# A two-layer sequence trunk: an addition moved into a transfer, one pair's order and last operand, and the places of one set of sums

## The chip, the cores and the metric

The kernel runs on one core of one Trainium2 chip. The core has five engines that work side by side, each through its own instructions in order: TensorE (PE in the profile; its weight loads are PEld), VectorE (DVE), ScalarE (ACT), GpSimd (POOL) and SyncE (SP). SP's queue only issues transfers (DMA) here; POOL issues others. The metric is the device time of one execution in microseconds (us). All numbers of a trace are from one profiled execution and count from the start of its span.

## What is computed

The reference runs two layers over x (512 tokens, width 2048, float32). Cut to what matters here:

```python
def hybrid_layer(x, w_in, w_out, ...):
    h = rmsnorm(x, g_pre)
    z = h @ w_in                      # 2048 x 7184
    gq, gk, gv, gg, ga, aq, ak, av, ag = split_columns(z)
    # gated linear attention on gq, gk, gv with gate ga; its output times silu(gg)
    # chunked softmax attention on aq, ak, av; its output times silu(ag)
    y = concatenate([o_gla, o_att]) @ w_out
    return x + rmsnorm(y, g_post)
```

Nearly all of the time goes into `h @ w_in` and the product with `w_out`.

## The kernel before

**Precision.** Every float32 operand is split into a high part (a cast on ScalarE, "wh" for weights) and a low part (the difference, on VectorE, "wl"); three matmuls, high x high, high x low and low x high, make one product. `Job.high` (line 211) casts, `Job.low` (line 232) subtracts at line 237. Token operands are split by `split` (cast at line 108, difference at line 109).

**Blocks and pairs.** The columns of `w_in` are cut into 14 blocks of 512 (AG1 and AG2 are 264 wide, with the gate's columns). A block is multiplied directly by `std_gemm` (a "standard" pass, kind "std", eight chunks of the contraction), or two blocks together by `fast_gemm`, which uses the seven products of a Strassen-Winograd scheme, P1 to P7, over four chunks c = 0 to 3. The names in the order lists are product and chunk: "50" is P5 of chunk 0. For a chunk c and a pair (b0, b1) the weights come from four blocks: P1 loads b0's upper block into H; P5 loads b1's upper block into r and makes H = H + r; P6 loads b1's lower block (b22) and makes H = H + b22; P3 uses b22; P7 makes r = H - r with b0's upper block; P2 and P4 use b0's lower block. The additions are at line 221, P7's subtraction at line 223. P1, P2 and P4 take tokens as their left operand, P5, P6, P3 and P7 take sums of tokens, S1, S2, S4 and S3 (the table `LEFT`).

**Sums of tokens.** `make_sums` makes S1 to S4 for each chunk out of the tokens' quarters a11, a12, a21, a22: S1 = a21 - a22 and S3 = a11 - a21 (by `sub`, line 599), S2 (line 622) and S4 (line 625). `put` splits a sum into a tile and writes it to DRAM from POOL (line 610). In layer two S1 and S2 have tiles of their own (`HOMES`), S3 and S4 rotate through three staging tiles, and in layer one S1 has tiles of its own and the other three rotate through five; a tile is used again when its store has left. `put` ties the split's cast behind the last cast emitted so far (`last_cast`). In layer one `behind` also ties every S1 and S3 subtraction behind the last operand split emitted (`ends[-1]`). A later pair reads its sums back from DRAM into "sa" tiles, a ring of four (line 206), from SP; so does P4 with the quarter called A22.

**Order.** All jobs of the kernel stand in one list, `stream`. `ahead` prepares them in front of TensorE: loads up to five jobs ahead, casts up to four, low parts three. Side work is a list of generators, `tasks`; `pump` advances it by one step, and `Pace` pumps `rate` steps at each call. `std_gemm` calls its pace once for each chunk and token tile, `fast_gemm` once for each product and chunk. The program's order gives priorities; a scheduler at build time, with its own model of times, then fixes each engine's order, and `tc.issue_after(x)` keeps an instruction behind x on its engine. Rings: weights wait in "raw" (five tiles), "H" (four), "wh" (four), "wl" (three).

**Around the change, layer two (l = 1).** The layer runs: the standard pass of AG0 for token tiles 0 and 1; P2 and P1 of the values' pair (AV0, AV1), `PROD_FRONT`; the standard pass of AG0 for token tiles 2 and 3, from about 860 to 882 us, in which the sums are pumped at a rate of 0.9; the rest of the values' pair, `PROD_REST`, to about 944 us; then the narrow pair (AG1, AG2), `PROD_GATE`, to about 989 us; then the pair of queries and keys. For the values' pair of layer two, `Job.parted` is true, and its H tiles are the slots g4 to g7. S1 and S2 are taken from their tiles in this pair and in the narrow one (`home`); S3, S4 and A22 are read from DRAM.

**Layer one (l = 0).** The tokens arrive transposed and unnormalised; `first_operands` scales and splits them on VectorE (until about 69 us) while the standard passes of AG0, AG1 and AG2 run. `token_sums` follows in the list of tasks, beside AG1 and AG2, and the values' pair follows at about 97 us. The four tiles of the "H" ring first hold tokens and are free for this pair's weights when a chunk's last sum is done.

Of the kernel before, what the change touches and what calls it, by code (L numbers as in the profile page):

```python
# [23 lines left out]
NB_IN = 14  # L24
# [12 lines left out]
def hybrid_trunk(  # L37
# [98 lines left out]
    def order(text):  # L136
        return [("P" + z[0], int(z[1])) for z in text.split()]
# [3 lines left out]
    PROD_OUT = order("10 20 11 21 12 13 50 51 60 61 22 23 52 53 62 63 30 31 32 33 70 71 72 73 40 41 42 43")  # L141
    PROD_FRONT = order("20 21 22 23 10 11 12 13")
    PROD_REST = order("50 51 52 53 60 61 30 62 63 31 70 32 71 72 73 33 40 41 42 43")
    PROD_GATE = order("10 11 50 12 51 13 52 60 53 61 30 62 31 63 32 70 33 71 20 72 21 73 22 23 40 41 42 43")
    GATE_PAIR = (AG1, AG2)
    LEFT = {"P5": "S1", "P6": "S2", "P3": "S4", "P7": "S3", "P4": "A22"}
    SPARE = ("g12", "g13", "g16", "g17")
# [3 lines left out]
    class Job:  # L151
# [23 lines left out]
        def load(self):  # L175
            k, c, p, b0, b1 = self.kind, self.c, self.pair, self.b0, self.b1
            end = b0 >= NB_IN and k != "std"
            if end:
                c = OC[c]
            top, bottom = (c + 4, c) if end else (c, c + 4)  # L180
            mid = end and b0 == W23[0] and self.l < L - 1
            if k == "std":
                self.raw = self.fetch(rtile("raw", bufs=5), b0, c)
            elif k == "P1":
                h = slot(f"g{4 + c}", [2, 512]) if self.parted else rtile("H")
                p["H", self.c] = self.fetch(h, b0, top)
                last_h[0] = last_load[0]
            elif k == "P5":
                p["r", self.c] = self.fetch(rtile("raw", bufs=5), b1, top)
            elif k == "P6":  # L190
                p["r", self.c] = p["b22", self.c] = self.fetch(rtile("raw", bufs=5), b1, bottom)
            elif k == "P7":
                p["r", self.c] = p.pop(("t", self.c), None) or self.fetch(rtile("raw", bufs=5), b0, top)
            elif k == "P2" or (k == "P4" and (end or self.parted)):
                p["r", self.c] = self.fetch(rtile("raw", bufs=5), b0, bottom)
            sums = (so_d if end else sa_d)[self.l]
            src = sums.get((LEFT.get(k), c))
            if self.l == L - 1:
                home = k in ("P5", "P6") and b0 in (AV0, AG1)
            else:  # L200
                home = k == "P5" and b0 == AV0
            if src is not None and b0 != NB_IN and not home:
                until(lambda: k == "P4" or (id(sums), LEFT[k], c) in written)
                self.a = rtile("sa", (2, 512), F32R)
                with tc.issue_after(last_h[0]) if mid else nullcontext():
                    last_load[0] = nc.sync.dma_start(flat(self.a), src).ins
            if b0 == W23[0] and k == ("P6" if mid else "P5"):
                with tc.issue_after(last_h[0]):
                    p["t", self.c] = self.fetch(slot(f"a11{self.c}" if mid else SPARE[self.c], [2, 512]), b0, c + 4)

        def high(self):
            k, c, p = self.kind, self.c, self.pair
            if k == "std":
                src = self.raw
            else:
                h, r = p["H", c] if k != "P2" else None, p.get(("b22" if k == "P3" else "r", c))
                src = h if k in ("P1", "P5", "P6", "P4") else r
                early = k in ("P7", "P4") and self.b0 == W23[0] and self.l < L - 1
                with tc.issue_after(lows[-4 if early else -2]) if self.b0 >= NB_IN else nullcontext():
                    if k in ("P5", "P6") or (k == "P4" and (self.b0 >= NB_IN or self.parted)):  # L220
                        nc.vector.tensor_tensor(out=h, in0=h, in1=r, op=ALU.add)  # L221
                    elif k == "P7":
                        nc.vector.tensor_tensor(out=r, in0=h, in1=r, op=ALU.subtract)  # L223
            self.src = src
            self.wh = self.cut(rtile("wh", dtype=F32R))
            for z in self.parts():
                last_cast[0] = nc.scalar.copy(self.wh[:, z, :], src[:, z, :]).ins  # L227
# [98 lines left out]
    def std_gemm(l, blk, outs, chunks, operand, evac, rate=0.0, skip=0, lag=0):  # L326
        wide = W if blk == AG0 else N1
        pss = {o: ps_mm.tile([P, W], F32, tag="mm", name=nm("mm"))[:, :wide] for o in outs}
        pace = Pace(rate, skip)
        outs, n = list(outs), len(chunks)  # L330
        order = [(i, o) for i in range(n - lag) for o in outs]
        order += [(i, o) for o in outs for i in range(n - lag, n)]
        jobs = {}
        for i, o in order:
            c = chunks[i]
            if i not in jobs:
                jobs[i] = take(l, blk, "std", c)
            job = jobs[i]
            a = operand(o // 2, c)
            for kk in range(2):  # L340
                t = slice(kk * 256 + (o % 2) * P, kk * 256 + (o % 2 + 1) * P)
                ops = ((0, job.wh), (0, job.wl), (1, job.wh))
                for m, (part, rhs) in enumerate(ops):
                    nc.tensor.matmul(  # L344
                        pss[o], a(part, kk, o) if callable(a) else a[:, part, t], rhs[:, kk, :],
                        start=(i == 0 and kk == 0 and m == 0),
                        stop=(i == n - 1 and kk == 1 and m == 2),
                    )
            if o == outs[-1] and (i < n - lag or i == n - 1):
                ahead()  # L350
            if i == n - 1:
                evac(o, pss[o])
            pace()
# [240 lines left out]
    def make_sums(dst, tags, parts, home={}, behind=None):  # L594
        stage = [0]

        def sub(out, a, b):
            with tc.issue_after(behind()) if behind else nullcontext():
                nc.vector.tensor_tensor(out=out, in0=a, in1=b, op=ALU.subtract)

        def put(name, c, src):
            if (name, c) in home:
                op = A[name, c] = slot(home[name, c], [2, 512], F32R)
            else:
                tag = tags[stage[0] % len(tags)]
                op = rtile(tag, dtype=F32R) if tag == "H" else slot(tag, [2, 512], F32R)
                stage[0] += 1
            with tc.issue_after(last_cast[0]):
                split(op[:, 0, :], op[:, 1, :], src)
            nc.gpsimd.dma_start(dst[name, c], flat(op))  # L610
            written.add((id(dst), name, c))

        for c in range(4):
            a11, a12, a21, a22 = parts(c)
            yield
            sub(a22, a21, a22)
            put("S1", c, a22)
            yield
            sub(a21, a11, a21)
            put("S3", c, a21)  # L620
            yield
            nc.vector.tensor_tensor(out=a22, in0=a22, in1=a11, op=ALU.subtract)
            put("S2", c, a22)
            yield
            nc.vector.tensor_tensor(out=a12, in0=a12, in1=a22, op=ALU.add)
            put("S4", c, a12)
            yield

    def token_sums(l):
        tags, home = (("g10", "g16", "H"), HOMES) if l else (STAGE, HOME)  # L630
        return make_sums(sa_d[l], tags, lambda c: (full[0, c][:, 0, :], full[0, c][:, 1, :], full[1, c][:, 0, :], full[1, c][:, 1, :]), home, None if l else lambda: ends[-1])

    VT = ("g16", "g17", "g4", "g5", "g6", "g7", "g12", "g13")
    V, U = {}, {}
# [133 lines left out]
    def layer(l):  # L768
# [136 lines left out]
        if l:  # L905
            std_gemm(l, AG0, (0, 1), CO, operand_in, gate_evac(0), rate=1.3)
            roles.reverse()
            acc = {n: [ps_mm.tile([P, W], F32, tag="mm", name=nm("mm")) for _ in range(2)] for n in "YX"}
            fast_gemm(l, PAIRS[0], av_consume, rate=2.5, prod=PROD_FRONT, acc=acc)
            until(lambda: all((kh, 1, c) in A for kh in range(2) for c in range(4)))  # L910
            tasks.append(token_sums(l))
            std_gemm(l, AG0, (2, 3), CO, operand_in, gate_evac(0), rate=0.9)
            fast_gemm(l, PAIRS[0], av_consume, rate=1, prod=PROD_REST, acc=acc)
            drain()
            fast_gemm(l, GATE_PAIR, gate_consume, prod=PROD_GATE)
            tasks.append(load_forget_gate(l))
            tasks.append(forget_gate())
            act_table("natural_log_exp_and_others")
        else:
            fast_gemm(l, PAIRS[0], av_consume, rate=0.5)  # L920
# [658 lines left out]
```

## Time and profile before

| | us |
|---|---|
| three runs of the kernel before | 1628.22, 1624.83, 1628.18 |
| their median | 1628.18 |
| the profiled execution | 1626.38 |
| its span, first to last instruction | 1624.6 |

A second table gives where TensorE was idle for more than half a microsecond at a time in the stages of the edits:

| at, us | idle, us | ended by |
|---|---|---|
| 119.27 | 4.83 | ScalarE's cast of a weight tile (layer one, values' pair) |
| 891.83 | 3.14 | VectorE's low part of a weight tile (layer two, values' pair) |
| 970.22 | 0.84 | a transfer of S into "sa" (narrow pair) |
| 986.75 | 3.00 | a transfer of A22 into "sa" (narrow pair) |
| 989.50 | 0.75 | ScalarE's cast of a weight tile (queries and keys) |

How to read the rows: a timeline row has start, length, engine, line, operation, the written tile, "<-", the read tiles, sizes and a count, and in brackets the engine's idle time before it and what ended it. Tiles go by their tags ("g", "sa", "H"), buffer numbers left out. "mm" and "ax" are accumulators. A row of the view by stretches gives its length, the busy time and count of PE, PEld, DVE, ACT and POOL, the granted clock of TensorE, the mean busy share of the DMA engines and what they moved in GB/s. A matmul's row covers its pipeline, so the rows of successive matmuls overlap; their starts give the rate.

### The profile page before, as it was taken

The page shows a single profiled execution, that of the slowest core. Times are in us where ns is not written, and L with a number is a line of the kernel's source. Part 1 is how long each engine was busy: PE and PEld are TensorE (multiplying, and loading weights), DVE is VectorE, ACT ScalarE, POOL GpSimd, SP SyncE. Part 2 cuts the span into 40 slices and gives each one's busy share as a digit, 9 for nine tenths or more (in the row PEclk, how much of TensorE's full clock was granted, in tenths as well). Part 3 has the DMA queues.
Part 4 walks back from the last instruction along what each step waited for, and adds up shares of the span by engine and source line. Part 5 has one row for each costly group of instructions (what it writes and reads, how often), then busy time and mean ns, then how long its engine had stood idle before and what let it go on. Part 6 is the DMA issues. An engine that isn't in the chain of part 4 may idle for free.

```text
span 1624.6 us, 25125 instructions
## 1 busy us (share of the span) xinstructions
PE 1600.1 (98%) x9158; PEld 1378.9 (85%) x9158; DVE 1284.1 (79%) x1701; ACT 921.8 (57%) x1535; POOL 129.8 (8%) x202
## 2 busy tenths in 40 slices
PE   9989999999999999999999999999999999999998
PEld 7978999998888777888887798999988877788886
DVE  5977768678677877998989877686786778789887
ACT  7544445657455556665785545456575545465655
POOL 0220000000000001100121000000100000101001
PEclk9999999999999999999999999999999999999999
DMA  9697777685767768689868968866958677686887
GB/s 348 222 403 247 266 270 236 214 302 184 270 217 270 272 216 316 220 310 384 307 244 318 381 233 317 287 219 225 320 207 283 214 268 271 218 312 231 330 305 209
DMA packets 137228, 441.39 MB, mean 272 GB/s; under 512 B 14884, under 2 KB 27428, under 8 KB 137072
## 3 DMA queue, kind: packets, MB, share of 16 engines
q1 hardware_dynamic: 120528, 379.96, 67.0%
q0 software_dynamic: 16288, 59.53, 10.0%
q8 instruction: 72, 1.18, 0.3%
q14 instruction: 52, 0.43, 0.1%
q10 hardware_dynamic: 288, 0.30, 0.1%
HBM read 380.20 MB, written 61.62 MB: 272 GB/s over the span
## 4 chain that ended last, share of the span: by engine, by line
PE 85%; DMA 5%; issue 4%; DVE 4%; ACT 1%; POOL 0%; POOLq 0%; SPq 0%; DVEq 0%; ACTq 0%
PE mm L431 50%; PE mm L421 18%; PE mm L344 5%; PE ax L431 3%; DMA raw<-in_w_dram 3%; PE ax L1000 2%; DVE wl L237 2%; PE ax L1186 1%; PE ax L983 1%; PE ax L1158 1%; DMA sa<-S 1%; PE ax L963 1%; PE ax L962 1%; PE ax L961 1%; DMA sa<-A 1%
## 5 line engine op out<-in xcount | busy, mean ns | idle before, releaser
L431 PE MATMUL mm<-wh,sa 128*128 128x512 f32 (+1 forms) x1632 | 517.6, 388 | 5.2 <-DMA sa<-A 3.0
L227 ACT CAST wh<-H 128x1024 fp32r<-128x1024 f32 (+1 forms) x256 | 261.5, 1024 | 212.5 <-PE mm L431 88.7
L237 DVE TENSOR_TENSOR wl<-H,wh 128x1024 fp32r<-128x1024 f32 (+1 forms) x256 | 303.5, 1188 | 97.6 <-PE mm L431 35.8
L431 PEld LDWEIGHTS mm<-wh,sa 128*128 128x128 f32 x1632 | 303.0, 188 | 76.2 <-issue 13.0
L227 ACT CAST wh<-raw 128x1024 fp32r<-128x1024 f32 (+2 forms) x237 | 236.3, 1002 | 210.3 <-PE mm L431 85.6
L237 DVE TENSOR_TENSOR wl<-raw,wh 128x1024 fp32r<-128x1024 f32 (+2 forms) x237 | 272.8, 1154 | 63.3 <-PE mm L431 26.9
L431 PE MATMUL mm<-wl,sa 128*128 128x512 f32 (+1 forms) x816 | 313.9, 385 | 0.3 <-DVE wl L237 0.3
L421 PE MATMUL mm<-sa,wh 128*128 128x256 f32 x1280 | 237.7, 285 | 0.0
L431 PE MATMUL mm<-wh,a 128*128 128x512 f32 (+1 forms) x672 | 219.8, 392 | 5.9 <-ACT wh L227 5.9
L421 PEld LDWEIGHTS mm<-sa,wh 128*128 128x128 f32 x1280 | 200.5, 191 | 0.5
L421 PE MATMUL mm<-sa,wl 128*128 128x256 f32 x640 | 181.4, 284 | 0.6 <-DVE wl L237 0.6
L431 PEld LDWEIGHTS mm<-wl,sa 128*128 128x128 f32 x816 | 153.5, 188 | 29.5 <-DVE wl L237 1.1
L221 DVE TENSOR_TENSOR H<-H,raw 128x1024 f32<-128x1024 f32 (+1 forms) x144 | 170.3, 1188 | 1.0
L431 PEld LDWEIGHTS mm<-wh,a 128*128 128x128 f32 x672 | 125.4, 189 | 32.0 <-ACT wh L227 7.0
L431 PE MATMUL mm<-wl,a 128*128 128x512 f32 (+1 forms) x336 | 131.1, 391 | 0.3 <-DVE wl L237 0.3
L421 PEld LDWEIGHTS mm<-sa,wl 128*128 128x128 f32 x640 | 122.5, 191 | 0.8 <-DVE wl L237 0.8
L431 PE MATMUL mm<-wh,g 128*128 128x512 f32 (+1 forms) x384 | 115.8, 378 | 0.4 <-ACT wh L227 0.4
L475 POOL TENSOR_TENSOR sm<-sm,mhalf 128x2 f32<-128x2 f32 (+2 forms) x40 | 49.4, 1235 | 697.1 <-DVE sm L1010 388.3
L223 DVE TENSOR_TENSOR raw<-H,raw 128x1024 f32<-128x1024 f32 (+1 forms) x56 | 66.4, 1186 | 45.0 <-DMA raw<-in_w_dram 42.8
L421 PE MATMUL mm<-a,wh 128*128 128x256 f32 x512 | 96.7, 289 | 0.8 <-ACT wh L227 0.8
L381 ACT COPY ev<-mm 128x512 f32<-128x512 f32 (+1 forms) x112 | 64.0, 571 | 54.9 <-PE mm L431 39.5
L243 DVE TENSOR_TENSOR H<-H,raw 128x1024 f32<-128x1024 f32 (+1 forms) x48 | 56.7, 1181 | 42.0 <-DMA raw<-in_w_dram 41.5
(272 smaller groups left out, 2406.6 us busy)
## 6 DMA issues: line engine op xcount, KB each, us to landing
raw<-in_w_dram SPq DMA_DIRECT2D x291, 512.0 KB, 4.9
sa<-S SPq DMA_DIRECT2D x188, 512.0 KB, 4.5
H<-in_w_dram SPq DMA_DIRECT2D x60, 512.0 KB, 5.2
sa<-A SPq DMA_DIRECT2D x52, 512.0 KB, 5.7
sa<-oS SPq DMA_DIRECT2D x32, 512.0 KB, 5.4
S<-g POOLq DMA_DIRECT2D x30, 512.0 KB, 8.0
raw<-in_w_ag_dram SPq DMA_DIRECT2D x32, 264.0 KB, 4.2
oS<-g POOLq DMA_DIRECT2D x16, 512.0 KB, 4.5
```

Of the source, the lines that this page charges most:

```text
L221: nc.vector.tensor_tensor(out=h, in0=h, in1=r, op=ALU.add)
L223: nc.vector.tensor_tensor(out=r, in0=h, in1=r, op=ALU.subtract)
L227: last_cast[0] = nc.scalar.copy(self.wh[:, z, :], src[:, z, :]).ins
L237: last_low[0] = nc.vector.tensor_tensor(out=self.wl[:, z, :], in0=self.src[:, z, :], in1=self.wh[:, z, :].bitcast(F32), op=ALU.subtract).ins
L243: nc.vector.tensor_tensor(out=h, in0=h, in1=self.src, op=ALU.add)
L344: nc.tensor.matmul(pss[o], a(part, kk, o) if callable(a) else a[:, part, t], rhs[:, kk, :], start=(i == 0 and kk == 0 and m == 0), stop=(i ...
L381: last_copy[0] = nc.scalar.copy(e, src[t]).ins
L421: nc.tensor.matmul(dst, lhs[:, kk, f], a[:, part, tok], start=(fresh and kk == 0 and m == 0 and ft % 2 == 0), stop=(c == 3 and kk == 1 and ...
L431: last_mm[0] = nc.tensor.matmul(out_ps[t], a[:, part, tok], rhs[:, kk, :], start=(fresh and kk == 0 and m == 0), stop=(c == 3 and kk == 1 ...
L475: nc.gpsimd.tensor_tensor(out=out_r, in0=v, in1=mhalf[:, : v.shape[-1]], op=ALU.pow)
L961: nc.tensor.matmul(ps[:, :n], self.qh[:, t], self.kh[:, :n], start=True, stop=False)
L1000: nc.tensor.matmul(o, self.pt[i][:, j * P : (j + 1) * P], av[hd // 4, j // 2][:, j % 2, (hd % 4) * P : (hd % 4 + 1) * P], start=(j == 0), ...
```

## The change

Five edits, all of them in the order and the means of the same arithmetic.

1. In layer two's values' pair P5 no longer loads its block into a raw tile for VectorE to add; POOL issues a transfer that reads the block from DRAM and adds it into the H tile (`accum_op=ALU.add`). `Job.high` skips the addition for it.
2. `PROD_GATE`, the order of the narrow pair's 28 jobs, alternates P1 with P5, P6 with P3 and P7 with P2.
3. With each P5 of layer two's narrow pair the chunk's A22 operand is loaded into g4 to g7, and P4 takes it from there; P4 loads no "sa" tile in this pair any more.
4. In layer one the S1 and S3 subtractions of chunk 0 are tied to nothing, those of chunk 1 to the third last operand split, those of chunks 2 and 3 to the last as before.
5. The rate at which layer two's second standard pass pumps the sums goes from 0.9 to 1.3.

```diff
-    PROD_GATE = order("10 11 50 12 51 13 52 60 53 61 30 62 31 63 32 70 33 71 20 72 21 73 22 23 40 41 42 43")
+    PROD_GATE = order("10 50 11 51 12 52 13 53 60 30 61 31 62 32 63 33 70 20 71 21 72 22 73 23 40 41 42 43")
...
+            elif k == "P5" and self.parted:
+                h = p["H", c]
+                src = w[self.l, b1 - (b1 > AG1), top].rearrange("p (k n) -> p k n", k=2)
+                nc.gpsimd.dma_start(h, src, accum_op=ALU.add)
             elif k == "P5":
                 p["r", self.c] = self.fetch(rtile("raw", bufs=5), b1, top)
...
-            if src is not None and b0 != NB_IN and not home:
+            if b0 == AG1 and k == "P5":
+                p["a22", c] = slot(f"g{4 + c}", [2, 512], F32R)
+                nc.sync.dma_start(flat(p["a22", c]), sums["A22", c])
+            if b0 == AG1 and k == "P4":
+                self.a = p["a22", c]
+            elif src is not None and b0 != NB_IN and not home:
...
-                    if k in ("P5", "P6") or (k == "P4" and (self.b0 >= NB_IN or self.parted)):
+                    if k == "P6" or (k == "P5" and not self.parted) or (k == "P4" and (self.b0 >= NB_IN or self.parted)):
                         nc.vector.tensor_tensor(out=h, in0=h, in1=r, op=ALU.add)
...
-        def sub(out, a, b):
-            with tc.issue_after(behind()) if behind else nullcontext():
+        def sub(c, out, a, b):
+            with tc.issue_after(behind(c)) if behind and c else nullcontext():
                 nc.vector.tensor_tensor(out=out, in0=a, in1=b, op=ALU.subtract)
...
-            sub(a22, a21, a22)
+            sub(c, a22, a21, a22)
...
-            sub(a21, a11, a21)
+            sub(c, a21, a11, a21)
...
-        return make_sums(sa_d[l], tags, lambda c: (...), home, None if l else lambda: ends[-1])
+        return make_sums(sa_d[l], tags, lambda c: (...), home, None if l else lambda c: ends[-3 if c == 1 else -1])
...
-            std_gemm(l, AG0, (2, 3), CO, operand_in, gate_evac(0), rate=0.9)
+            std_gemm(l, AG0, (2, 3), CO, operand_in, gate_evac(0), rate=1.3)
```

More of the change, by code (lines that the diff above doesn't have):

```diff
@@ L630, in token_sums @@
         tags, home = (("g10", "g16", "H"), HOMES) if l else (STAGE, HOME)
-        return make_sums(sa_d[l], tags, lambda c: (full[0, c][:, 0, :], full[0, c][:, 1, :], full[1, c][:, 0, :], full[1, c][:, 1, :]), home, None if l else lambda: ends[-1])
+        return make_sums(sa_d[l], tags, lambda c: (full[0, c][:, 0, :], full[0, c][:, 1, :], full[1, c][:, 0, :], full[1, c][:, 1, :]), home, None if l else lambda c: ends[-3 if c == 1 else -1])
     VT = ("g16", "g17", "g4", "g5", "g6", "g7", "g12", "g13")
```

## The prediction

> **What bounds the kernel now.** I read the head of the page, then stretches of layer two's start, then what TensorE waited for in them.
>
> ```profile
> span 1624.6 us, 25125 instructions
> ...
> PE 1600.1 (98%) x9158; PEld 1378.9 (85%) x9158; DVE 1284.1 (79%) x1701; ACT 921.8 (57%) x1535; POOL 129.8 (8%) x202
> ```
>
> TensorE is the bound: it is idle for 24.5 us in all. No matmul is added or removed, so the change can win only idle time and the slow clock behind it. The stages of layer two's edits (columns: length; busy time of PE, PEld, DVE, ACT, POOL; granted clock; DMA share; GB/s):
>
> ```profile
> 840.00:862.00 22.00, 22.00 (x109) 18.47 (x107) 19.18 (x25) 17.41 (x32) 2.14 (x4) 1.00 0.56 209
> 862.00:880.00 18.00, 18.00 (x81) 14.89 (x81) 15.71 (x18) 10.52 (x13) 3.19 (x6) 1.00 0.89 288
> 880.00:910.00 30.00, 26.64 (x107) 20.72 (x106) 28.45 (x33) 16.43 (x25) 6.40 (x12) 0.94 1.02 387
> 910.00:944.00 34.00, 33.70 (x154) 27.47 (x153) 24.79 (x26) 13.04 (x16) 0.26 (x1) 1.00 0.97 363
> ...
> 960.00:1000.00 40.00, 35.38 (x266) 34.41 (x266) 28.89 (x53) 21.72 (x36) 4.92 (x9) 0.91 0.97 376
> ```
>
> **Stall A**, in the values' pair (880 to 910): 30.00 - 26.64 = 3.4 us idle, and 0.06 x 30 = 1.8 us lost to the clock: 5.2 us. **Stall B**, at the end of the narrow pair (960 to 1000): 4.6 us idle and 0.09 x 40 = 3.6 us of clock: 8.2 us. TensorE's rows name what ended them, in brackets behind the idle time:
>
> ```profile
> 891.83 0.50 PE L431 MATMUL mm<-wl,g 128*128 128x512 f32 x1 [3.14 <-DVE wl L237]
> ...
> 986.75 0.36 PE L431 MATMUL mm<-wh,sa 128*128 128x264 f32 x1 [3.00 <-DMA sa<-A]
> ...
> 989.50 1.22 PE L421 MATMUL mm<-a,wh 128*128 128x256 f32 x4 [0.75 <-ACT wh L227]
> ```
>
> In A VectorE is late; in B narrow P4's last operand, and after it the next pair's first cast. Layer one has a larger hole, **stall C**:
>
> ```profile
> 115.00:120.00 5.00, 0.73 (x2) 0.50 (x2) 0.75 (x1) 1.82 (x2) 0.00 (x0) 0.75 1.03 420
> 120.00:125.00 5.00, 5.00 (x15) 3.77 (x14) 4.95 (x5) 2.31 (x4) 0.00 (x0) 0.56 0.78 282
> ```
>
> That is 4.3 us idle and (0.25 + 0.44) x 5 = 3.4 us of clock, 7.7 us.
>
> **The addition by transfer** takes four additions (line 221) from VectorE and four loads from SP's queue, and gives POOL four accumulating transfers.
>
> ```profile
> 868.03 1.23 DVE L221 TENSOR_TENSOR g<-g,raw 128x1024 f32<-128x1024 f32 x1 [1.01 <-DMA raw<-in_w_dram]
> 869.17 0.69 DVE L109 TENSOR_TENSOR g<-g,g 128x512 fp32r<-128x512 f32 x1
> 869.77 0.68 DVE L625 TENSOR_TENSOR H<-H,g 128x512 f32<-128x512 f32 x1
> ```
>
> From start to start a wide operation takes 1.14 us and a half one 0.60, so 4 x 1.14 = 4.6 us leave VectorE, and the wait of 1.0 us for the first load with them. VectorE is the engine that is late in A, busy 28.45 of 30 us. The trace has no accumulating load. The nearest rows are the accumulating stores at the kernel's end (issue in ns, then landing in us: least, median, most). The outer ends are the plain stores A<-sa of 840 to 862 us and S<-g of 85 to 122 us, where the transfers were full:
>
> ```profile
> L1431 POOL DMA_DIRECT2D out_dram<-a x2: 852/893/934, 1602.3 to 1609.1; - x2
> DMA to landing us min/median/max: 5.4/5.8/7.7
> DMA to landing us min/median/max: 2.9/2.9/3.2
> DMA to landing us min/median/max: 10.3/13.7/15.4
> ```
>
> A landing takes 2.9 to 15.4 us; I take 5.8, the same kind of transfer. The four tiles are free once P1's low parts are made, before the standard pass, and P5 reads them after it: eight chunks of 12 matmuls at 18.00/81 = 0.222 us, 21 us. From 840 to 862 us POOL is busy 2.14 of 22 us and the transfers 0.56: 22 x 209 = 4.6 MB, of 9.3 MB that the 420 GB/s above would move. Even counted twice (4.2 MB) the additions fit. Cost: nothing, hidden by the standard pass. If they are issued only among the sums' stores, P5's first cast is up to 15.4 - 5.8 = 9.6 us later. The Trainium skill, "SBUF — State Buffer" (SBUF: two separate sides), speaks against moving loads to POOL: VectorE's two-port modes keep GpSimd from writing descriptors, and in its example 620 ns become 3100. By that four transfers would take POOL some 10 us longer, an estimate, and the sum would lose up to 10 us; the row above, 0.9 us to issue, shows no such growth, and the sum keeps nothing of it.
>
> **The rate of 1.3.** Sixteen paces pump 20.8 steps in place of 14.4, so five sums (S4 of chunk 2, all of chunk 3) come before the pair's rest: 5 splits and 3 additions, 8 x 0.60 = 4.8 us of VectorE, moved forward. Against it stand the 4.6 us taken out and 18.00 - 15.71 = 2.3 us idle at 862 to 880, so it fits. It also ends a knot: `put` ties a sum's cast behind the last cast emitted, four products ahead. P5's last product needs chunk 3's S1, which so far came behind the cast of P3's first product; now it comes behind that of P5's third. What tightens is staging, three tiles for eight S3 and S4. ScalarE waited once for a store to leave, while stores landed in (second row) 7.1 us:
>
> ```profile
> 882.39 0.62 ACT L108 CAST g<-g 128x512 fp32r<-128x512 f32 x1 [2.31 <-DMA S<-g]
> DMA to landing us min/median/max: 3.7/7.1/8.5
> ```
>
> Such waits may recur; casts run three products (8 us) ahead, which covers them. Of A's 5.2 us I count 4.1 as won, and set 1.6 us against new small waits in a stage whose transfers are 0.97 to 1.02 busy. Bounds: 5.2 won, 10 lost.
>
> **The narrow pair.** P4's four operands leave the ring of "sa" tiles for g4 to g7, which the values' P4 frees with its low parts; SP's issue waits for the last of these, then loads 40 us earlier than now:
>
> ```profile
> 934.92 1.21 DVE L237 TENSOR_TENSOR wl<-g,wh 128x1024 fp32r<-128x1024 f32 x1
> 976.52 0.33 SPq L206 DMA_DIRECT2D sa<-A  x1
> 977.20 3.10 SPq L172 DMA_DIRECT2D H<-in_w_dram  x3
> DMA to landing us min/median/max: 10.5/11.4/12.7
> 988.41 1.04 ACT L227 CAST wh<-H 128x1024 fp32r<-128x1024 f32 x1
> ```
>
> The 2.1 MB (5.0 us at 420 GB/s) now load near 936 us. Queued behind them on SP are narrow P5's and P6's weights, due products later. They vanish from in front of the next pair's H tiles, whose landing (fourth row) falls from 10.5 to 5.5 us: 977.2 + 5.5 + 1.04 of cast = 983.7 us. TensorE, without the 4.6 - 0.75 = 3.9 us lost before 988.75 us, would be through at 984.9. So the next late thing is that H tile, just in time. I keep 1.5 us of idle and clock: 6.7 us won (bounds 0 and 8.2). Alternating P1 with P5 and P7 with P2 moves no work, and one product still lies between each eviction and the next writer of its bank; it costs nothing beside a VectorE that is busy 28.89 of 40 us.
>
> **The untied subtractions.** Four half operations, 2.4 us, may pass VectorE's last operand splits. Stall C's chain:
>
> ```profile
> 106.02 0.62 ACT L108 CAST g<-H 128x512 fp32r<-128x512 f32 x1 [2.93 <-DMA S<-g]
> 108.45 0.33 SPq L172 DMA_DIRECT2D H<-in_w_dram  x1
> 119.27 1.22 PE L431 MATMUL mm<-wh,a 128*128 128x512 f32 x2 [4.83 <-ACT wh L227]
> ```
>
> The last sum waits for a staging store, then TensorE for the H tile that the sum frees. Earlier sums of chunks 0 and 1 put stores ahead of the jam, but a VectorE that is nearly full lets little through. Bounds: 2.4 us lost, 7.7 won; I take 1.5 won, nearer to nothing.
>
> **Sum.** -4.1 + 1.6 - 6.7 - 1.5 = -10.7 us. The profiled execution took 1626.4 us (1.8 beside the span); the runs are 1624.83 to 1628.22, median 1628.18. 1626.4 - 10.7 = 1615.7, and 0.8 for the higher median: **1616.5**.
>
> **Rivals.** *Layer one's hole closes too* (0.12): stores moved out of the jam shorten two landings in a row, and C gives 6 more: about 1610. For: 420 GB/s there, nothing to spare. Against: VectorE is full before it.
>
> *Only the narrow pair wins* (0.16): A moves to staging or a late operand; -6.7 + 1 gives 1621.
>
> *The transfers bind* (0.12): 862 to 944 us moved 18 x 288 + 30 x 387 + 34 x 363 = 29.1 MB. If the 363 GB/s of the last stretch is all there is, that takes 80 of the 82 us, nothing shrinks, and the time is 1625. Against: 420 GB/s in layer one, at which it takes 69 us. The Trainium skill, "SBUF — State Buffer" (A bandwidth-pool intuition that's wrong), gives some 358 GB/s between HBM and a core; by that this rival would be the result, at about 81 us. The 387 and 420 speak against it.
>
> *Slower* (0.14): the sums outrun staging, and ScalarE, which works in order, holds the casts behind them. S3 of chunk 3 reuses a tile after two stores, the first at 865.56 us; P5's fourth cast may stand behind it and is due three products (8.0 us) after P5's start:
>
> ```profile
> 865.56 0.53 POOL L610 DMA_DIRECT2D S<-g  x1 [9.22 <-DVE g L109]
> 881.99 0.39 PE L431 MATMUL ax<-wl,g 128*128 128x512 f32 x1
> ```
>
> The cast is done at 865.6 + 2 x (landing + 1.5) + 1.6 against 890.0. At 7.1 us nothing waits, at 15.4 TensorE waits 11.0 us, at 18, with the additions in the same queue, 16.2, each plus 2 of clock. A, B and C together lose 5.2 + 6.7 + 1.5 = 13.4, so it is slower from 15.6 us on; at 18 it gives +4.8, 1632. Against: 7.1 here.
>
> Only the untied edit can fail to act (C unchanged, 1.5 us).
>
> **Numbers.** Forecast 0.46, its own range 1612 to 1621. 0.2%, 3.3 us, is about what a measurement can tell from no change. Faster: 0.46 + 0.12 + 0.15 of the narrow-only case = 0.73; same 0.13; slower 0.14. Range 1609 to 1628, from the closed hole to no gain; the slower case and 0.04 below stay out.
>
> **What would show it.** Accumulating loads on POOL before 862 us and P5's additions gone from line 221; no wait on wl near 890; no sa<-A at the narrow end, the next cast within 1 us; S<-g landings near 8 us. Landings of 15 us, or additions issued among the sums' stores, would make it wrong.

## The result and the profile after

| | us |
|---|---|
| the changed kernel, median of eight runs | 1618.3 (1616.13 to 1621.13) |
| the kernel before beside it, median of eight | 1625.26 (1622.78 to 1628.22) |
| ratio | 0.9956, 95% interval 0.9944 to 0.9968 |
| the profiled execution of the changed kernel | 1617.69, span 1615.9 |

It is faster by 7 us (5.2 to 9.1 us by the interval); the forecast was 1616.5 in 1609 to 1628. From one profiled span to the other it is 1624.6 - 1615.9 = 8.7 us. In the changed kernel lines stand nine further down once the additions are passed: 221 is 230, 227 is 236, 237 is 246, 421 is 430, 431 is 440, 206 is 215.

The view by stretches of the changed kernel (columns as before: length; busy time of PE, PEld, DVE, ACT, POOL; granted clock; DMA share; GB/s):

```profile
100.00:125.00 25.00, 20.36 (x80) 15.10 (x79) 18.22 (x17) 10.87 (x14) 2.20 (x4) 0.93 0.90 361
...
840.00:862.00 22.00, 22.00 (x107) 18.41 (x106) 20.18 (x26) 16.73 (x29) 5.75 (x8) 1.00 0.95 251
862.00:880.00 18.00, 18.00 (x81) 14.93 (x80) 15.71 (x20) 11.47 (x17) 4.81 (x9) 1.00 1.01 396
880.00:910.00 30.00, 29.66 (x130) 23.90 (x129) 26.77 (x29) 16.64 (x23) 5.10 (x10) 1.00 1.02 385
910.00:944.00 34.00, 34.00 (x185) 29.54 (x184) 26.38 (x32) 14.50 (x20) 0.00 (x0) 1.00 0.91 348
...
960.00:1000.00 40.00, 35.56 (x277) 34.74 (x276) 31.49 (x52) 20.38 (x31) 4.91 (x9) 0.96 0.84 310
```

Set these beside the rows of before. Stall A is gone: 0.3 us idle at 880 to 910 in place of 3.4, the clock 1.00 in place of 0.94. Stall B is not: 4.4 us idle at 960 to 1000 in place of 4.6. What ends it is another thing; TensorE's longest waits over the whole span (the view of waits: us in total, times, longest):

```profile
PE mm L440 <- ACT wh L236: 5.1, 6, 3.3
PE mm L430 <- ACT wh L236: 3.9, 1, 3.9
```

The 3.0 us for sa<-A have left the list. The 3.9 us on line 430 are new: the query and key pair's first product waits for the cast of its first H tile. The 3.3 on line 440 is layer one's stall C, 4.8 before.

### The profile page after: what moved, and what is told of

Same layout as the page of the kernel before. It is cut to its first block, busy times and chain, and to the rows that moved or that the text cites. A ratio compares the mean times of both kernels' runs of the same rounds, so it can differ in the third digit from the quotient of the medians.

```text
span 1615.9 us, 25135 instructions
## 1 busy us (share of the span) xinstructions
PE 1595.7 (99%) x9158; PEld 1377.2 (85%) x9158; DVE 1279.2 (79%) x1697; ACT 920.6 (57%) x1535; POOL 134.9 (8%) x206
## 4 chain that ended last, share of the span: by engine, by line
PE 87%; DMA 4%; issue 4%; DVE 3%; ACT 1%; POOL 1%; POOLq 0%; SPq 0%; DVEq 0%; ACTq 0%
PE mm L440 51%; PE mm L430 19%; PE mm L353 5%; PE ax L440 3%; PE ax L1009 2%; DMA H<-in_w_dram 2%; DMA raw<-in_w_dram 2%; PE ax L1195 1%; DVE wl L246 1%; PE ax L992 1%; PE ax L1167 1%; PE ax L972 1%; PE ax L971 1%; PE ax L970 1%; DMA S<-g 0%
## 5 line engine op out<-in xcount | busy, mean ns | idle before, releaser
L440 PE MATMUL mm<-wh,sa 128*128 128x512 f32 (+1 forms) x1600 | 510.3, 390 | 1.7 <-DMA sa<-S 1.1
L440 PEld LDWEIGHTS mm<-wh,sa 128*128 128x128 f32 x1600 | 297.7, 188 | 71.3 <-issue 7.7
L440 PE MATMUL mm<-wl,sa 128*128 128x512 f32 (+1 forms) x800 | 309.3, 387 | 0.0
L440 PE MATMUL mm<-wh,g 128*128 128x512 f32 (+1 forms) x416 | 120.5, 368 | 0.5 <-ACT wh L236 0.4
```

Source lines behind the costliest of these rows:

```text
L440: last_mm[0] = nc.tensor.matmul(out_ps[t], a[:, part, tok], rhs[:, kk, :], start=(fresh and kk == 0 and m == 0), stop=(c == 3 and kk == 1 ...
```

## The experiments

All kernels compute the same result; only the order, the means or the place of work differ. Each ratio is against the kernel before on the same chip.

### The parts of the values' pair, and the first layer, each alone

**The addition by transfer alone** (edit 1):

```diff
+            elif k == "P5" and self.parted:
+                h = p["H", c]
+                src = w[self.l, b1 - (b1 > AG1), top].rearrange("p (k n) -> p k n", k=2)
+                nc.gpsimd.dma_start(h, src, accum_op=ALU.add)
...
-                    if k in ("P5", "P6") or (k == "P4" and (self.b0 >= NB_IN or self.parted)):
+                    if k == "P6" or (k == "P5" and not self.parted) or (k == "P4" and (self.b0 >= NB_IN or self.parted)):
```

> Edit 1 alone: only P5's addition by transfer, everything else as before. Theory 1 (the four additions on VectorE were what made it late): TensorE's idle time in the values' pair of layer two, 3.4 us before and 0.3 us with the whole change, falls to 1 us or less, ratio about 0.997. Rival (the knot: chunk 3's S1 was emitted behind the cast of P3's first product, whatever VectorE has to do): 2.5 us or more of it stays, ratio 0.999 to 1.0. Both: the accumulating loads are issued before 862 us and land in 3 to 8 us.

Measured 1621.22, ratio 0.9973 (0.9964 to 0.9983). The view by stretches of that kernel:

```profile
880.00:910.00 30.00, 29.57 (x131) 24.17 (x130) 26.21 (x29) 18.39 (x25) 5.86 (x11) 1.00 1.02 385
...
960.00:1000.00 40.00, 33.87 (x254) 32.90 (x253) 27.44 (x50) 19.08 (x32) 4.93 (x9) 0.91 0.95 365
```

Stall A's idle time goes with this edit alone, 0.4 us in place of 3.4, and the rival falls. The clock reads 1.00 here in place of 0.94, but it also reads 1.00 in the profiles of edit 5 alone and of edit 4 alone (below), which keep 1.8 and 3.8 us of idle time in these 30 us; that the clock's 1.8 us hang on the stall is not shown. The four loads are issued from 843.9 to 855.4 us and land in 5.5 to 9.4 us, a little later than the 3 to 8 expected. At the narrow end 6.1 us are idle in this profile in place of 4.6, and the wait for sa<-A is 4.0 us, 3.0 before. The two later kernels with this edit and the old narrow pair have 4.3 and 4.2, so that the stall is handed on is not shown.

**The rate alone** (edit 5):

```diff
-            std_gemm(l, AG0, (2, 3), CO, operand_in, gate_evac(0), rate=0.9)
+            std_gemm(l, AG0, (2, 3), CO, operand_in, gate_evac(0), rate=1.3)
```

> Edit 5 alone: the sums at a rate of 1.3, P5 still adds on VectorE. Theory 1: 4.8 us of sums come in front of an already late VectorE, so the idle time in the values' pair stays at 3 us or grows to 5, ratio 1.0 to 1.002. Rival (the knot): the idle time falls to 1 us or less, ratio about 0.997.

Measured 1625.01, ratio 0.9999 (0.9986 to 1.0012): nothing. The stretches:

```profile
880.00:910.00 30.00, 28.18 (x121) 21.82 (x120) 28.93 (x33) 17.67 (x24) 6.41 (x12) 1.00 1.02 384
910.00:944.00 34.00, 32.34 (x147) 26.19 (x146) 24.22 (x25) 13.00 (x17) 0.26 (x1) 1.00 0.95 358
```

Idle time from 880 to 944 us is 1.82 + 1.66 = 3.5 us, against 3.4 + 0.3 before: the stall is cut in two and moved, and the rival (the knot) falls.

**Both** (edits 1 and 5, as in the two diffs above):

> Edits 1 and 5 together, without the narrow pair's and without layer one's. Both theories: idle time in the values' pair about 0.3 us as in the whole change, some 5 us with the clock; whether the narrow pair hands it on is open: its operand transfers then meet the same jam earlier. Ratio about 0.997; near 1.0 if the stall only moves to the narrow pair's end (idle there above 6 us).

Measured 1619.57, ratio 0.9961 (0.9949 to 0.9972), and the idle time at 880 to 910 is 30.00 - 29.89 = 0.1 us. The interval overlaps that of the addition alone, so the rate's share, 1.7 us by the medians, is not settled.

**The untied subtractions alone** (edit 4):

```diff
-        def sub(out, a, b):
-            with tc.issue_after(behind()) if behind else nullcontext():
+        def sub(c, out, a, b):
+            with tc.issue_after(behind(c)) if behind and c else nullcontext():
...
-home, None if l else lambda: ends[-1])
+home, None if l else lambda c: ends[-3 if c == 1 else -1])
```

> Edit 4 alone: layer one's subtractions of chunks 0 and 1 untied. If the hole at 100 to 125 us shrank through this edit, its idle time is 4.6 us in place of 6.6, the queries' and keys' pair starts at 182.6 us in place of 184.5, and the new idle 0.6 us at 50 to 75 us is there too; ratio about 0.999. Rival: layer one's gain is not this edit's, idle stays at 6.6 us, ratio 1.0.

Measured 1622.62, ratio 0.9991 (0.9978 to 1.0003), some 1.5 us with an interval that just holds zero; the medians lie 3.0 us apart. The stretch of layer one, the kernel before and then this one:

```profile
100.00:125.00 25.00, 18.41 (x67) 13.01 (x66) 18.22 (x19) 9.74 (x13) 3.28 (x6) 0.86 0.98 390
```

```profile
100.00:125.00 25.00, 21.19 (x79) 15.61 (x78) 18.10 (x20) 11.03 (x13) 2.64 (x5) 0.86 0.93 373
```

TensorE works 21.19 of these 25 us, 18.41 before: 2.8 us less idle. Some goes back at 50 to 75 us, where a new wait of 0.6 us for an activation of ScalarE stands (line 344, before the sums' stage). The queries' and keys' pair of layer one starts at 183.6 us, 184.4 before: 0.8 us in this profile, less than the 1.9 expected. All profiles together settle what the interval leaves open: without edit 4 (the kernel before and the runs of edit 1, of edit 5, of both and of edits 2 and 3) that pair starts at 184.3 to 185.5 us, and in the seven profiles with it at 182.0 to 183.6. The means are 2.1 us apart, so the edit wins about 2 us.

### The narrow pair

**Edits 2 and 3 alone:**

```diff
-    PROD_GATE = order("10 11 50 12 51 13 52 60 53 61 30 62 31 63 32 70 33 71 20 72 21 73 22 23 40 41 42 43")
+    PROD_GATE = order("10 50 11 51 12 52 13 53 60 30 61 31 62 32 63 33 70 20 71 21 72 22 73 23 40 41 42 43")
...
+            if b0 == AG1 and k == "P5":
+                p["a22", c] = slot(f"g{4 + c}", [2, 512], F32R)
+                nc.sync.dma_start(flat(p["a22", c]), sums["A22", c])
+            if b0 == AG1 and k == "P4":
+                self.a = p["a22", c]
```

> The kernel before with the alternation and the A22 loads into free slots alone. Theory (the next pair's S1 loads and raws take the place of the A22 loads ahead of its H tiles): the waits sa<-A (3.0 us) go, a wait on the cast of the next pair's first H tile of 3 to 4.5 us stands in their place, 960 to 1000 us keeps 4 to 5 us of idle time, the H tiles land in 11 to 13 us, and the time is within 0.2% of before (1622 to 1627). Rival (the prediction's step: H lands in 5.5 us, 6.7 us won): idle time there under 1.5 us, 1619 or less. The idle time at 880 to 910 stays near 3.4 us by both.

Measured 1625.09, ratio 0.9993 (0.9984 to 1.0002). TensorE's rows and the stretch:

```profile
991.43 0.74 PE L426 MATMUL mm<-a,wh 128*128 128x256 f32 x4 [3.20 <-ACT wh L232]
```

```profile
960.00:1000.00 40.00, 35.80 (x282) 35.17 (x281) 28.94 (x55) 22.45 (x39) 5.04 (x10) 0.96 0.91 331
```

No wait on sa<-A is left; one of 3.2 us on the next pair's first cast stands in its place, and 4.2 us are idle. The theory held.

**The changed kernel without them** (the same two pieces put back):

> The changed kernel with the narrow pair put back (the old alternation, A22 loaded into the ring as before); the addition by transfer, the rate and the untied subtractions stay. Theory (the narrow edits do win something once the pair before them runs ahead, though less than 6.7 us): waits of 1.5 to 4 us on sa<-A and sa<-S at 960 to 1000 us, the query-key pair starts at 983 to 985 us in place of 981, and the time is 1619 to 1621.5, 2 to 3.5 us above the changed kernel. Rival (they win nothing, as alone): within 1 us of the changed kernel, 1617 to 1618.7.

Measured 1618.02, ratio 0.9946 (0.9930 to 0.9962); the changed kernel, run once more on another chip, has 0.9951. The rival held: the narrow pair's two edits win nothing in the changed kernel either. Its stretch and its longest wait there (1.0 us more stand on sa<-S):

```profile
960.00:1000.00 40.00, 35.76 (x273) 35.33 (x273) 29.19 (x50) 20.98 (x32) 4.92 (x9) 0.91 0.91 350
```

```profile
PE mm L435 <- DMA sa<-A: 3.2, 1, 3.2
```

4.2 us idle with the edits taken out, 4.4 with them in. Only the name of the last comer differs.

### What took the place of the A22 loads

SP's queue says why. In the kernel before, with A22 in the ring of "sa" tiles (timeline of SP: start, length until the last of x is issued, what):

```profile
974.63 1.46 SPq L172 DMA_DIRECT2D raw<-in_w_dram  x2
976.52 0.33 SPq L206 DMA_DIRECT2D sa<-A  x1
977.20 3.10 SPq L172 DMA_DIRECT2D H<-in_w_dram  x3
980.65 0.33 SPq L206 DMA_DIRECT2D sa<-S  x1
```

The query and key pair's S1 loads (sa<-S) come behind its H loads, since P4's operands hold the ring. In the changed kernel:

```profile
961.84 0.39 SPq L215 DMA_DIRECT2D sa<-S  x1
963.46 1.05 SPq L172 DMA_DIRECT2D raw<-in_w_dram  x2
964.61 0.38 SPq L215 DMA_DIRECT2D sa<-S  x1
966.55 1.56 SPq L172 DMA_DIRECT2D raw<-in_w_dram  x2
968.17 0.42 SPq L215 DMA_DIRECT2D sa<-S  x1
968.69 0.39 SPq L172 DMA_DIRECT2D raw<-in_w_dram  x1
969.17 0.39 SPq L172 DMA_DIRECT2D H<-in_w_dram  x1
969.67 0.42 SPq L215 DMA_DIRECT2D sa<-S  x1
```

The ring is free, and three of the four S1 loads, 1.6 MB that the second product wants, go out ahead of the first H tile, which the first product wants. The four A22 loads that left were 2.1 MB. The chain of waits of the changed kernel (start, length, what) goes through that H tile:

```profile
968.05 0.96 PE mm L440 x8
...
969.17 10.56 DMA H<-in_w_dram
...
979.82 1.05 ACT wh L236
```

To test it, **S1 is tied behind the H loads**, the changed kernel otherwise:

```diff
-                with tc.issue_after(last_h[0]) if mid else nullcontext():
+                later_s1 = self.l == L - 1 and b0 == QK01 and k == "P5"
+                with tc.issue_after(last_h[0]) if mid or later_s1 else nullcontext():
                     last_load[0] = nc.sync.dma_start(flat(self.a), src).ins
```

> The changed kernel, with the S1 loads of layer two's first query-key pair (4 loads of 512 KB) tied behind the loads of that pair's H tiles. Theory (they displaced H): the first H load is issued several us earlier or lands in 8 us or less in place of 12.3, the wait of the first product on its first cast falls from 3.9 us to 0 to 2, the idle time at 960 to 1000 us from 4.4 to 1 to 3 us, and the time is 2 to 4 us under that of the changed kernel (1614 to 1616.5 beside it). Rival (the four raw tiles ahead of H, or the traffic as a whole, set its landing): the wait stays at 3 us or more and the time within 1.5 us of the changed kernel. Second rival: S1 becomes late for the pair's second product, with a wait sa<-S of 2 us or more, and the time is the same.

Measured 1611.39 (four runs), ratio 0.9906 (0.9893 to 0.9919). The changed kernel beside it on the same chip:

> The changed kernel once more beside the two before, for a comparison on one chip: 0.9956 of the kernel before, 0.9944 to 0.9968; the first cast of the query-key pair 3.5 to 4.5 us late, H landing in 12 to 13 us.

Measured 1617.71, ratio 0.9951 (0.9939 to 0.9964), first cast 4.2 us late. The intervals lie apart: the tie wins 6.3 us over the changed kernel (1617.71 - 1611.39), by the medians, more than the 2 to 4 expected. This kernel's SP queue, stretch and first product:

```profile
961.84 4.81 SPq L172 DMA_DIRECT2D raw<-in_w_dram  x5
966.95 1.75 SPq L172 DMA_DIRECT2D H<-in_w_dram  x2
968.75 0.42 SPq L216 DMA_DIRECT2D sa<-S  x1
```

```profile
960.00:1000.00 40.00, 39.48 (x326) 39.10 (x326) 34.10 (x53) 24.20 (x36) 4.92 (x9) 1.00 0.87 314
```

```profile
975.13 0.74 PE L431 MATMUL mm<-a,wh 128*128 128x256 f32 x4
```

The first product of the narrow P4, the changed kernel and then this one:

```profile
970.78 0.28 PE L440 MATMUL mm<-wh,g 128*128 128x264 f32 x1
```

```profile
968.96 0.29 PE L441 MATMUL mm<-wh,g 128*128 128x264 f32 x1
```

The landing of that pair's H tiles, in the same order:

```profile
DMA to landing us min/median/max: 12.0/12.3/12.6
```

```profile
DMA to landing us min/median/max: 7.3/8.6/10.0
```

No bracket stands behind the first product: it waited for nothing, and it starts at 975.1, against 980.9 in the changed kernel (5.8 earlier) and 989.5 before. Of the 5.8 us this profile was ahead by 1.8 at the narrow P4 already, ahead of the wait that the tie ends; the other 4.0 are that wait. The H tiles land in 8.6 us (median) in place of 12.3. No wait on sa<-S stands among TensorE's waits there, so the second rival falls too. Idle time at 960 to 1000 falls from 4.4 to 0.5 us, and the clock goes from 0.96 to 1.00 (0.91 in the second profile of the changed kernel): 3.9 us of idle and up to 1.6 of clock, 0.04 x 40.

**The raw tiles behind H too:**

```diff
             elif k == "P5":
-                p["r", self.c] = self.fetch(rtile("raw", bufs=5), b1, top)
+                with tc.issue_after(last_h[0]) if self.l == L - 1 and b0 == QK01 else nullcontext():
+                    p["r", self.c] = self.fetch(rtile("raw", bufs=5), b1, top)
```

> As the one before, with the raw tiles of that pair's P5 tied behind the H tiles too. Theory: H has the queue for itself, lands in 5 to 7 us, the wait on the first cast is under 1 us and the idle time at 960 to 1000 us under 2 us; the time is 3 to 5 us under that of the changed kernel if the raws still come in time, and as the changed kernel if P5's additions now wait 3 us or more for them (VectorE, H<-H,raw behind DMA raw). Rival (traffic as a whole): the wait stays at 3 us or more.

Measured 1612.46, ratio 0.9912 (0.9900 to 0.9925), no better: the interval overlaps that of S1 alone behind H. The stall was gone with the raw tiles still ahead of H, so they were not what made it. The H loads start only at 971.62, when their tiles come free. Most of that delay is not the tie's: this profile runs 4.4 us behind the one before already, its narrow P4 starting at 973.4 us. But the queue that the raw tiles would have used is empty until then; the stretch shows a DMA share of 0.69, where S1 behind H alone has 0.98:

```profile
960.00:980.00 20.00, 19.62 (x160) 19.19 (x159) 15.68 (x36) 11.68 (x23) 3.26 (x6) 1.00 0.69 224
```

**S1 behind H, the old order of the narrow jobs** (edit 2 put back):

> The kernel with S1 behind the H tiles (1611.4), with the old order of the narrow pair's jobs. Theory (the alternation costs and wins nothing): idle time at 960 to 1000 us under 1.5 us, the time within 1.5 us of that kernel, 1610 to 1613. Rival (the alternation is what brings the pair's casts and sums forward): a wait of 2 us or more at the narrow pair or at the next pair's first cast, 1613.5 or more.

Measured 1613.71, ratio 0.9914 (0.9895 to 0.9933), idle time at 960 to 1000 0.7 us. The median lies over the expected 1613 and just within the rival's range. But the interval of the alternating order (on another chip) lies almost wholly inside this one, and no wait of 2 us shows in the pair: that the alternation matters is not shown. Its stretch:

```profile
960.00:1000.00 40.00, 39.26 (x323) 38.70 (x322) 34.46 (x55) 23.02 (x36) 4.92 (x9) 1.00 0.92 344
```

Four kernels as a table of the narrow end:

| A22 loaded | S1 against H | idle 960 to 1000, us | median, us |
|---|---|---|---|
| into the ring, late | behind | 4.2 | 1618.0 |
| into free slots, early | ahead | 4.4 | 1617.7 and 1618.3 |
| into free slots, early | behind | 0.5 | 1611.4 |
| the same, old order | behind | 0.7 | 1613.7 |

Either half alone leaves the stall; both together end it. In the first row S1 is behind H without a tie, since P4's operands hold the ring.

One span of time leaves out what happened earlier in a profile: from P5's first product in layer two's values' pair (881.99 us before) to the first product of its queries and keys (989.50 before). All profiles fall into three groups:

| kernels | that span, us |
|---|---|
| P5's addition on VectorE (before; edit 4; edit 5; edits 2 and 3) | 107.5, 106.9, 106.6, 106.1 |
| addition by transfer, S1 not tied (edit 1; edits 1 and 5; without 2 and 3; all five, twice) | 103.0, 102.7, 101.8, 101.1, 101.2 |
| all five, and S1 tied (the tie; raw tied too; old order) | 96.6, 98.7, 97.2 |

The groups lie apart. Between single profiles of the first two the rate moves the span by under 1 us, and the narrow pair's edits by at most 1.4.

## Why the prediction was right in sum, and wrong in one step

**Direction and time held, the parts did not.** The prediction's sum was 2.5 from A (4.1 less 1.6 for new waits), 6.7 from B and 1.5 from C. By the runs it is 4.4 from A with the addition alone (2.8 to 5.9 by the interval) and 6.3 with the rate (4.6 to 8.3), nothing from B that the runs can tell from zero, and about 2 from C. The win was 7.0 us and not 10.7: A gave more than its 2.5, B nothing of its 6.7, and the two errors cancel in part. That the time came within 1.8 us of the forecast is luck beyond that. The forecast counted from 1626.4 + 0.8 = 1627.2 (no working is given for the 0.8; the median stood 1.8 over the profiled execution), and the kernel before, run beside the changed one, has 1625.26, which is 1.9 less.

**The step that failed** is the one on the narrow pair: the A22 loads "vanish from in front of the next pair's H tiles, whose landing (fourth row) falls from 10.5 to 5.5 us". They did vanish, and sa<-A no longer ends a wait. Yet the sign set beside it, "the next cast within 1 us", did not come: that cast is 3.9 us late. The first H tile came 10.56 us after its issue, as late as before. The prediction asked which loads leave the queue and not which ones the freed ring of "sa" tiles lets in. It named the right late thing, "that H tile, just in time", and gave it 3.9 us too little. The run without the narrow edits (1618.02) shows that this term was worth nothing; the run with S1 behind H shows that the prediction's mechanism, a shorter queue ahead of H, does give nearly what was claimed for it, 6.3 of 6.7 us, with H landing in 8.6 us and not 5.5.

**A was right in mechanism and small in size.** VectorE was late, and four additions taken off it were enough: the addition alone ends the stall's idle time. Of its 3.4 us the changed kernel keeps 0.3, the clock reads 1.00, and the 1.6 us set against new small waits did not come in this pair. Staging stayed calm: ScalarE waited once for a store to leave, 2.8 us at 862 to 910, and TensorE for that cast only 0.2 us. The prediction's clock terms are somewhat large, since they count the slow clock over time in which TensorE was idle: with busy time alone, C's two rows give 0.25 x 0.73 + 0.44 x 5 = 2.4 us in place of 3.4.

**The accumulating load** was hidden, as forecast: TensorE is busy 22.00 of the 22 us in which the transfers run. The view of its line (ns to issue: least, median, most; then us to land):

```profile
L191 POOL DMA_DIRECT2D g<-in_w_dram x4: 867/872/920, 841.3 to 852.8; - x4
...
DMA to landing us min/median/max: 5.5/7.5/9.0
```

I took 5.8 us to land and 0.9 to issue; it is 7.5 and 0.87. VectorE is busy 20.18 of 22 us beside it, and the issue does not grow. The growth that the prediction weighed from the Trainium skill is not seen here. The Trainium skill's same page, "SBUF — State Buffer" (Who interferes with whom), limits it: an addition or subtraction of two tiles has no two-port mode, and takes only the shared read side, not the write side that descriptors need (the Trainium skill marks this last step as inferred). VectorE's rows from 840 to 862 us are all of that kind, so the Trainium skill's page as a whole agrees with the 0.87 us, and I had weighed a rule that does not reach this stretch. Nor do the transfers bind: 862 to 880 us moves 396 GB/s in place of 288, so the work was pulled into a stretch with room, and 910 to 944 falls to a share of 0.91.

**The rate's "knot"** was claimed and is not shown: alone the rate moves the waits and wins nothing, and beside the addition its part is within the error. The addition alone ends the idle time with the sums still pumped at 0.9, so the knot was not what held TensorE up.

**C** came out as predicted in size. Idle time at 100 to 150 us goes from 6.6 to 4.6 us in the changed kernel, the first product of layer one's queries and keys from 184.4 to 182.5 us: 1.9 us against the 1.5 predicted, and 2.1 over all profiles. VectorE lets little through, as argued, and the rival of a closed hole falls: 3.3 us for a cast remain.

Of the other rivals, *only the narrow pair wins* came out the other way round, and *slower*, by staging, had no landing near 15.6 us to stand on: the sums' stores of 860 to 912 us land in 4.8 to 9.1.

## What to carry to other kernels

When loads are taken out of a ring of buffers, list what that ring will fetch next, and in which place of the queue it will be issued: the freed tiles pull later loads forward, past the one that is due first. Here the stall was won only when the next thing due was also issued ahead of the loads due after it, which one tie could force. And test each half of a joint edit with the other present and absent: the narrow pair's edits won nothing that the runs could measure, alone and in the changed kernel, and were one of the two conditions of a gain of 6 us.

## What the hardware showed that was not expected

A stretch with accumulating loads keeps the transfer engines busy for far longer than its bytes say. The queues of 840 to 862 us (packets, MB, share of 16 engines), the kernel before and then the changed one; q0 holds POOL's transfers:

```profile
q0 software_dynamic: 653, 2.35, 27.6%
```

```profile
q0 software_dynamic: 1122, 4.12, 78.8%
```

With the four accumulating loads this queue moves 1.77 MB more (the loads are 2.1 MB; 0.25 of the 2.35 MB before were neither these nor the four stores). It takes (0.788 - 0.276) x 22 = 11.3 us more of all the engines, 6.4 us for a MB; the transfers before took 0.276 x 22 / 2.35 = 2.6. The run of edit 1 alone shows the same, with 3.92 MB and 74.8%. By all queues the changed kernel has a share of 0.95 here at 251 GB/s, where the next 18 us move 396 GB/s at 1.01. The transfers beside the loads land later, the stores A<-sa in 7.4 us (median) in place of 2.9 and the weights that SP loads into raw tiles in 7.8 in place of 3.9. The shares add up the time that packets took, and the stores' packets may take longer beside the loads, so how much of the 11.3 us is the accumulation's own and how much the stores' is not separated. The addition was free in this place since the transfers had a share of only 0.56; it is now 0.95. What the same edit does in a stretch that is already full was not tried.
